# Expert stages: rows of the tokens fetched by index for six of eight pairs of experts, weights in 8 KB pieces, the long conditional inside the sixth pair

## The chip, the cores and the metric

One core of a Trainium2 chip runs the whole program in one launch. The metric is the device time of that launch in microseconds (us). TensorE multiplies, VectorE and ScalarE do the elementwise work and empty the PSUM banks, POOL (GpSimd) does a little of it and starts some DMAs, SP starts the DMAs of the weights. In the profile PE is TensorE, PEld its weight load, DVE VectorE, ACT ScalarE; a name with a q (SPq, PEldq) is the engine's sequencer.

## The reference, cut to what matters

Two transformer blocks of two layers each on 256 tokens of width 1024, all in fp32. The first block's layers end in a mixture of experts; the second block's contain a cross attention to 256 memory tokens with four heads of 64.

```python
def grouped_moe(h, router_w, router_b, w_gate, w_up, w_down):
    scores = sigmoid(t @ router_w)              # 256 tokens x 16 experts, 4 groups of 4
    ...                                         # best group by its top two, then top two experts in it
    top_w = top_s / sum(top_s);  combine = ...  # weight of each expert for each token
    for e in range(16):
        he = silu(t @ w_gate[e]) * (t @ w_up[e])            # 1024 -> 512
        y = y + combine[:, e:e + 1] * (he @ w_down[e])      # 512 -> 1024
```

## The kernel before

**Expert stage** (`moe`, once per layer). The 16 experts are taken as 8 pairs, p = 0 to 7 ("first" to "eighth pair"). All weights of a pair are loaded, 12 pieces of 1 MiB: four each for gate, up and down (`weights`, L1520; `fetch`, L220). Each piece fills one buffer of 128 partitions x 2048 numbers. `fetch` spreads 128 consecutive rows over the partitions, so a partition's 8 KB come in four rows of 2 KB (gate, up) or two of 4 KB (down). 17 buffers take turns; SP issues the DMAs in order and waits for the buffer that comes next to be free. When the stage starts, the buffers are full.

Only tokens that chose an expert are worked on, up to 64 per expert in the main path. From the ranks of the tokens `hot` (L1330) builds a matrix of zeros and ones (tokens x places). `gather` (L1344) picks the tokens on TensorE: the normalised rows, split into a high part `xh` and a low part `xl`, times that matrix, for two pairs at once, column block by column block; ScalarE applies the norm's scale A and bias B on the way out into `hg`. `prepare` (L1379) does it for pairs 0, 2, 4, 6; for pair 0 in two halves, the other times at the end of the pair before.

`up` (L1385) then multiplies `hg` with gate and up weights into banks `pg`, `pu`, two experts side by side in 64 columns each; adds the pair before back to the residual `x` (`self.pending`, four scatters of two matmuls); turns the places (`places`, L1359: `pS`, `pw`); forms silu(pg) * pu in `hd`, transposes it (`hT`, `hidT`). `down` (L1424) multiplies with the down weights into `po`, scales on VectorE and splits into `eo`, which the next pair scatters.

From the third pair on, a count per pair is read into registers, and two conditionals (L1545 ahead of `up`, L1548 ahead of `down`) take the next 32 tokens per expert (`more_up`, `more_down`), with a gather of their own. A conditional is a unit for TensorE, VectorE and ScalarE: each of them branches, drains and goes on.

For tokens beyond that there is one long conditional, `rounds` (L1509), in five nested levels with all experts' code in each. It stands ahead of the eighth pair, between the issue of its gate and up weights and that of its down weights, and SP takes part in it, since it issues DMAs inside.

**Router** (`router`, L1196) prepares weights for the router at the end of each mixer. **Cross attention** (`cross`, L2095, once per layer of the second block) works in steps over two pairs of heads: scores and exp, transposes of the scores (`cpT`), output (`co`, tokens on the partitions). After both, VectorE scales by the softmax sums (`rs`), and `rows_T` transposes the result (`trr`) for the output projection (`op`).

The order within an engine is set by a planner that simulates the engines at build time; calls in `pin` keep their order.

Of the kernel before, what the change touches and what calls it, by code (L numbers as in the profile page):

```python
# [11 lines left out]
F32 = mybir.dt.float32  # L12
# [53 lines left out]
def shape_constants():  # L66
# [15 lines left out]
        ("sum32", i[:, None] % 32 == np.arange(32)[None, :]),  # L82
        ("slots", np.tile(np.arange(1, 257), (P, 1))),
# [36 lines left out]
class Net:  # L120
# [519 lines left out]
    def start(self):  # L640
# [8 lines left out]
        self.one = self.gp.tile([P, 1], F32, name="one")  # L649
        self.rw = self.gp.tile([P, KD, NE], F32, name="rw")  # L650
# [31 lines left out]
    def vectors(self, ap):  # L682
# [7 lines left out]
        yield  # L690
        small(v2[0:96, :], I["sandwich_g_2"].rearrange("l s (k p) -> (l s k) p", p=P))
# [504 lines left out]
    def router(self, l):  # L1196
# [3 lines left out]
        A, B = self.scale_shift(l, 1)  # L1200
        rwa = self.sp.tile([P, KD, NE], F32, tag="gt", name="rwa")
# [12 lines left out]
    def moe(self, l):  # L1214
# [4 lines left out]
        with self.phase(f"moe{l}", MOE_RING, True) as mp:  # L1219
# [32 lines left out]
            def parts(t):  # L1252
                for c in range(2):
                    sl = (slice(None), t, slice(512 * c, 512 * c + 512))
                    pin(nc.scalar.copy(xh[sl], xn[sl]))
                    pin(nc.gpsimd.tensor_tensor(xl[sl], xn[sl], xh[sl].bitcast(F32), op=ALU.subtract))
            for t in range(2):
                for k0 in (0, 4):
                    self.norm_cols(self.norm_turn(self.x, t, k0), hT, t, k0)
                rs[t] = self.norm_rows(self.x, t, xn, t)  # L1260
            parts(0)
# [7 lines left out]
            parts(1)  # L1269
            sel = mp.tile([P, 2, 16], F32, name="sel")  # L1270
# [73 lines left out]
            def gather(oh, hg, k0=0, k1=KD):  # L1344

                n = hg.shape[2]
                per = min(512 // n, 4)
                for b0 in range(k0, k1, per):
                    ph = self.bank([P, per, n], name="ph")
                    for b in range(per):  # L1350
                        for i, (t, xx) in enumerate(((0, xh), (0, xl), (1, xh), (1, xl))):
                            pin(mm(ph[:, b, :], xx[:, t, 128 * (b0 + b):128 * (b0 + b) + 128], oh[t],
                                   start=i == 0, stop=i == 3))
                    for b in range(per):
                        k = b0 + b
                        nc.scalar.activation(hg[:, k, :], ph[:, b, :], AF.Identity,
                                             scale=A[:, k:k + 1], bias=B[:, k:k + 1])
# [21 lines left out]
            def prepare(p, k1=KD):  # L1379

                hg = self.sp.tile([P, KD, 256], F32, tag="xn", name="hg", bufs=1)
                self.first = hot((p, p + 1), 0, 64), hg
                gather(*self.first, 0, k1)

            def up(p, W):  # L1385

                new = p == 0
                if new:
                    prepare(0, 4)
                oh, hg = self.first  # L1390
# [3 lines left out]
                for w, pp in ((W[0], pg), (W[1], pu)):  # L1394
                    for k in range(KD):
                        if new and w is W[0] and k == 4:
                            gather(oh, hg, 4, 8)
                        for j in range(2):
                            pin(mm(pp[64 * j:64 * j + 64, :], hg[:, k, q][:, 64 * j:64 * j + 64], w[j][k // 4][:, k % 4, :],  # L1399
                                   start=k == 0, stop=k == KD - 1, tile_position=(0, 64 * j)))  # L1400

                if self.pending:
# [4 lines left out]
                V.tensor_tensor(hd, hd, pu, op=ALU.mult)  # L1407
                pt = self.bank([P, 4, P], name="hT")
                for k in range(4):
                    self.tr(pt[:, k, :], hd[:, 128 * k:128 * k + 128])  # L1410
                hidT = self.sp.tile([P, 4, P], F32, tag="e2", name="hidT")
                V.tensor_copy(hidT, pt)
                if p in (1, 3, 5):
                    prepare(p + 1)
                return hidT, Sm, ws
# [8 lines left out]
            def down(W, hidT, Sm, ws, last=False):  # L1424
# [13 lines left out]
                def back(n=4):  # L1438
# [20 lines left out]
            def more_up(p, r, W, hidT):  # L1459


                oh = hot((p,), 32 + 32 * r, 32)
                hg = self.sp.tile([P, KD, 64], F32, tag="e1", name="hga")
                gather(oh, hg)
                pp = self.bank([P, 512], name="pgu")
                for gu in ((0, 1),) if W else ((0,), (1,)):
                    w = W[:2] if W else [weights(src, 512, p, self.spare) if c in gu else None
                                         for c, src in enumerate(("exp_w_gate", "exp_w_up"))]
                    for k in range(KD):
                        for c in gu:  # L1470
                            for j in range(2):
                                i = 2 * c + j
                                mm(pp[32 * i:32 * i + 32, :], hg[:, k, 32 * j:32 * j + 32], w[c][j][k // 4][:, k % 4, :],
                                   start=k == 0, stop=k == KD - 1, tile_position=(0, 32 * i))
# [3 lines left out]
                Sm, ws = places([twice[:, t].rearrange("p c s -> p (c s)") for t in range(2)], p, r)  # L1478
                hd = self.sp.tile([P, 512], F32, tag="gt", name="hda")
                nc.scalar.copy(hd, pp)  # L1480
                pt = self.bank([P, 4, P], name="hT")
                for k in range(4):
                    self.tr(pt[:, k, :], hd[:, 128 * k:128 * k + 128])
# [4 lines left out]
            def more_down(p, W, hidT, Sm, ws):  # L1488
                po = self.bank([P, 512], name="po")
                w = W[2] if W else weights("exp_w_down", 256, p, self.spare)  # L1490
                for k in range(4):
                    for i in range(4):
                        j, c = i % 2, i // 2
                        mm(po[32 * i:32 * i + 32, :], hidT[:, k, 32 * j:32 * j + 32],
                           w[j][k // 2][:, k % 2, 512 * c:512 * c + 512], start=k == 0, stop=k == 3,
# [13 lines left out]
            def rounds(r):  # L1509

                with tc.If(left > 32 + 32 * r):
                    for rr, pp in [(1, e) for e in range(FIRST if r == 2 else 0)] + [(r, e) for e in range(8)]:
                        hidT = self.sp.tile([P, 4, 64], F32, tag="e2", name="hidTa")
                        more_down(pp, None, hidT, *more_up(pp, rr, None, hidT))
                    if r < 6:
                        rounds(r + 1)

            engines = (mybir.EngineType.PE, mybir.EngineType.DVE, mybir.EngineType.Activation)

            def weights(src, step, p, into=None):  # L1520
# [4 lines left out]
                t = [self.fetch(raw, w[j][k0:k0 + step, :]) for raw, (j, k0) in zip(into, cut)]  # L1525
                return t[0::2], t[1::2]

            for p in range(8):
                W = [weights("exp_w_gate", 512, p), weights("exp_w_up", 512, p)]
                self.spare = [self.slot([P, 2048]) for i in range(4)]  # L1530
                if p == 7:
                    left = nc.values_load(cnti[0:1, 0:1], min_val=0, max_val=2 * S,
                                          engines=engines + (mybir.EngineType.SP,))
                    rounds(2)
# [808 lines left out]
```

## Time and profile before

| | us |
|---|---|
| median of 3 runs | 1602.48 (1601.62 to 1604.23) |
| profiled execution, its own time | 1602.07 |
| its span | 1600.3 |
| TensorE busy | 1504.7 (94%) |
| VectorE busy | 887.1 (55%) |
| E0: first gate product to last scatter | 212.8 to 466.7 |
| E1: first gate product to last scatter | 622.3 to 856.0 |

Times inside the execution are counted from the span's start. A busy TensorE can hide small waits, since ends of matmuls are modelled. The DMA share is the time of all packets over 16 DMA engines and can pass 1, since packets overlap a little. The more_up path runs once, in E0's fourth pair.

### The profile page before, as it was taken

To read this page: it belongs to the slowest core of one execution; us is meant where nothing else is said; L and a number is where in the kernel's file an instruction comes from. 1 tells how busy PE (TensorE), PEld (TensorE's weight loads), DVE (VectorE), ACT (ScalarE), POOL (GpSimd) and SP (SyncE) were. 2 spreads that over 40 slices of the span, in tenths; PEclk is the share of its full clock that TensorE was granted. 3 is DMA by queue.
4 is the path that set the end of the run, shared out by engine and by line. 5 is a ranking of instruction groups with operands and counts; after the bars stand their busy time and mean duration, and the time that the engine had idled before them with its cause. 6 is when DMAs were issued, how large, how long until landed. Compare 5 with 4: busy or idle time off the path is not lost. (4 is left out here: it accounts for less than half of the span.)

```text
span 1600.3 us, 23014 instructions
## 1 busy us (share of the span) xinstructions
PE 1504.7 (94%) x8845; PEld 1072.0 (67%) x8845; DVE 887.1 (55%) x1704; ACT 679.6 (42%) x1421; POOL 121.4 (8%) x170
## 2 busy tenths in 40 slices
PE   6999999999789999999978999999999999999998
PEld 3766644444349975444425887888887997888887
DVE  3755531122248984222116786766667776766666
ACT  3434421111035653101105355665556666665554
POOL 0320010000000002000001100110000211110000
PEclk9999999999889999999989999999999999999999
DMA  9998999989968799999998632554655542545640
GB/s 357 345 314 294 344 396 391 391 315 393 347 215 273 276 328 366 397 391 392 394 340 277 182 106 93 162 194 162 220 171 161 163 150 84 186 157 186 210 158 27
DMA packets 225758, 412.30 MB, mean 258 GB/s; under 512 B 7705, under 2 KB 91313, under 8 KB 225617
## 3 DMA queue, kind: packets, MB, share of 16 engines
q1 hardware_dynamic: 223040, 403.46, 71.1%
q0 software_dynamic: 2304, 6.98, 1.4%
q8 instruction: 86, 1.41, 0.4%
q14 instruction: 56, 0.45, 0.1%
q10 hardware_dynamic: 272, 0.00, 0.0%
HBM read 409.35 MB, written 1.06 MB: 256 GB/s over the span
## 5 line engine op out<-in xcount | busy, mean ns | idle before, releaser
L229 DVE TENSOR_TENSOR hl<-w,hl 128x1024 fp32r<-128x1024 f32 x280 | 337.2, 1237 | 49.8 <-ACT hl L228 49.4
L228 ACT CAST hl<-w 128x1024 fp32r<-128x1024 f32 x280 | 280.3, 1046 | 33.0 <-DMA w<-in_even_w_in 19.6
L2218 PE MATMUL pgu<-hT,hl 128*128 128x512 f32 x640 | 224.3, 394 | 0.0
L2219 PE MATMUL pgu<-hT,hl 128*128 128x256 f32 x640 | 177.1, 277 | 0.0
L380 PE MATMUL lin<-hl,hThi 128*128 128x256 f32 (+2 forms) x480 | 158.8, 334 | 2.0 <-ACT hl L228 1.3
L381 PE MATMUL lin<-hl,hThi 128*128 128x256 f32 (+2 forms) x480 | 153.6, 321 | 1.9 <-DVE hl L229 1.7
L382 PE MATMUL lin<-hl,hTlo 128*128 128x256 f32 (+2 forms) x480 | 153.1, 320 | 0.4 <-DVE hTlo L557 0.4
L2218 PEld LDWEIGHTS pgu<-hT,hl 128*128 128x128 f32 x640 | 119.9, 187 | 27.8
L1399 PE MATMUL pg<-w,hg 128*64 128x512 f32 x512 | 118.6, 615 | 19.7 <-ACTq L1545 9.2
L1407 DVE TENSOR_TENSOR hd<-hd,pu 128x512 f32<-128x512 f32 x16 | 11.0, 688 | 225.9 <-PE pu L1399 225.9
L1432 PE MATMUL po<-w,hidT 128*64 128x512 f32 x512 | 113.6, 595 | 10.0 <-DVEq L1548 5.8
L2219 PEld LDWEIGHTS pgu<-hT,hl 128*128 128x128 f32 x640 | 120.2, 188 | 2.0
L1399 PE MATMUL pu<-w,hg 128*64 128x512 f32 x512 | 114.9, 593 | 1.9 <-DMA w<-in_exp_w_up 1.9
L380 PEld LDWEIGHTS lin<-hl,hThi 128*128 128x128 f32 x480 | 92.3, 192 | 17.6 <-issue 8.1
L1399 PEld LDWEIGHTS pg<-w,hg 128*64 128x64 f32 x512 | 40.9, 141 | 93.4 <-issue 69.5
L381 PEld LDWEIGHTS lin<-hl,hThi 128*128 128x128 f32 x480 | 92.2, 192 | 11.0 <-DVE hl L229 3.5
L382 PEld LDWEIGHTS lin<-hl,hTlo 128*128 128x128 f32 x480 | 92.1, 192 | 8.0 <-issue 1.7
L1399 PEld LDWEIGHTS pu<-w,hg 128*64 128x64 f32 x512 | 41.1, 137 | 72.7 <-issue 68.0
L1432 PEld LDWEIGHTS po<-w,hidT 128*64 128x64 f32 x512 | 40.4, 137 | 72.8 <-issue 59.5
L1444 DVE SCALAR_TENSOR_TENSOR of<-po,ws,gate 128x512 f32<-128x512 f32 x32 | 23.9, 748 | 104.5 <-PE po L1432 100.6
L1447 ACT CAST eo<-of 128x512 fp32r<-128x512 f32 x32 | 19.8, 617 | 124.7 <-DVE of L1444 124.4
L380 PE MATMUL linc<-hThi,hl 128*128 128x256 f32 x224 | 66.8, 298 | 0.0
(554 smaller groups left out, 2915.0 us busy)
## 6 DMA issues: line engine op xcount, KB each, us to landing
w<-in_exp_w_gate SPq DMA_DIRECT2D x64, 1024.0 KB, 14.9
w<-in_exp_w_down SPq DMA_DIRECT2D x64, 1024.0 KB, 14.2
w<-in_exp_w_up SPq DMA_DIRECT2D x64, 1024.0 KB, 14.2
w<-in_ada_w SPq DMA_DIRECT2D x48, 1024.0 KB, 7.1
w<-in_ffn_wg SPq DMA_DIRECT2D x22, 1024.0 KB, 5.5
w<-in_ffn_wu SPq DMA_DIRECT2D x22, 1024.0 KB, 7.3
w<-in_ffn_wd SPq DMA_DIRECT2D x22, 1024.0 KB, 8.9
w<-in_even_w_in SPq DMA_DIRECT2D x14, 1024.0 KB, 10.1
```

What stands on the lines that cost most here:

```text
L228: pin(self.nc.scalar.copy(w[:, 0], src))
L229: pin(self.nc.vector.tensor_tensor(w[:, 1], src, w[:, 0].bitcast(F32), op=ALU.subtract))
L380: pin(mm(out, lh, rh, start=start, stop=False))
L381: pin(mm(out, lh, rl, start=False, stop=False))
L382: pin(mm(out, ll, rh, start=False, stop=stop))
L1399: pin(mm(pp[64 * j:64 * j + 64, :], hg[:, k, q][:, 64 * j:64 * j + 64], w[j][k // 4][:, k % 4, :], start=k == 0, stop=k == KD - 1, tile_po ...
L1407: V.tensor_tensor(hd, hd, pu, op=ALU.mult)
L1432: pin(mm(po[c][64 * j:64 * j + 64, :], hidT[:, k, 64 * j:64 * j + 64], W[2][j][k // 2][:, k % 2, 512 * c:512 * c + 512], start=k == 0, sto ...
L1444: V.scalar_tensor_tensor(of, po[c], ws, gate[:, cs], op0=ALU.mult, op1=ALU.mult)
L1447: nc.scalar.copy(eh[c], of)
L2218: mm(pp[i], wh[:, k, :], both[:, :, k, :], start=k == 0, stop=False)
L2219: mm(pp[i][:, 0, :], wl[:, k, :], hi[:, k, :], start=False, stop=k == KD - 1)
```

## The change

1. `fetch` gets the pattern of rows as an argument. Expert weights use `(p k) n -> p k n`: a partition gets consecutive rows, 8 KB in one piece. The contraction index is permuted accordingly: `xh`, `xl`, the hidden columns and A, B (as `self.ab`) are read with a stride.
2. For pairs 0 and 1 `gather` stays. The normalised rows are written to HBM (`xd`, 1 MiB, from POOL). 24 matmuls of one column turn ranks into token numbers (`indices`), and POOL fetches rows by these numbers for pairs 2 to 7 (`rows`: 128 rows for the main path, 64 for more_up, 4 KB each). `columns` transposes them, with scale and bias on ScalarE (one half) and VectorE (the other).
3. In `up` two of the four scatters come ahead of the hidden transposes, two after them, then `places`, then `columns` for the next pair.
4. `rounds` goes; `rest` takes its place: one conditional, not nested, with a loop over all 16 experts and both halves of the tokens. It stands in the sixth pair, between the gate and up products and the scatters, behind the issue of the seventh pair's gate and up weights. Its limit is the one of before: 96 tokens for an expert, 64 in the first two pairs.
5. `router` moves A and B to the permuted order: 16 products with 32 x 4 results.
6. Cross attention scales the scores ahead of their transposes and forms the output with its columns on the partitions: 8 products of 64 x 256 in place of 16 of 128 x 64, no `rows_T`.

```diff
-    def fetch(self, raw, src):
-        self.nc.sync.dma_start(raw, src.rearrange("(k p) n -> p k n", p=P))
+    def fetch(self, raw, src, rows="(k p) n -> p k n"):
+        self.nc.sync.dma_start(raw, src.rearrange(rows, p=P))
...
+        for k in range(4):
+            for j in range(4):
+                nc.tensor.matmul(ps[32 * j:32 * j + 32, k, :], pick[:, k, :], v[:, :, :, j].rearrange("p i b -> p (i b)"),
+                                 start=True, stop=True, tile_position=(0, 32 * j))
...
+                    src = xn[sl].rearrange("p (q k) -> p k q", k=4)
+                    pin(nc.scalar.copy(hi, src))
+                    pin(nc.gpsimd.tensor_tensor(lo, src, hi.bitcast(F32), op=ALU.subtract))
...
+            nc.gpsimd.dma_start(xd.rearrange("(t p) d -> p t d", p=P), xn)
...
+            def indices():
+                px = self.bank([P, 16], name="px")
+                for p in range(2, 8):
+                    h, q = (p - 2) // 3, (p - 2) % 3
+                    for c, n, col in ((0, 128, p), (128, 64, 8 + p)):
+                        for t in range(2):
+                            mm(px[0:n, col:col + 1], ones_of[2 * h + t][:, q, c:c + n], self.tok[:, t:t + 1],
+                               start=t == 0, stop=t == 1)
...
+                rows(0, 2)
+                rows(0, 3)
+                rows(1, 2)
+            def rows(i, p):
+                n = 64 if i else 128
+                nc.gpsimd.indirect_dma_start(got[i][0:n, p % 2, :], None, xd[:, :],
+                                             bass.IndirectOffsetOnAxis(ap=idx[0:n, 8 * i + p:8 * i + p + 1], axis=0))
+            def columns(src, n, out):
+                src = src.rearrange("r (b q k) -> r b k q", b=2, k=4)
+                for b in range(2):
+                    pt = self.bank([P, 4, n], name="hgT")
+                    for k in range(4):
+                        self.tr(pt[:, k, :], src[:, b, k, :])
+                    if b:
+                        o = out[:, 4:8, :]
+                        V.tensor_tensor(o, pt, self.ab[:, 0, b, :].unsqueeze(2).to_broadcast([P, 4, n]), op=ALU.mult)
+                        V.tensor_tensor(o, o, self.ab[:, 1, b, :].unsqueeze(2).to_broadcast([P, 4, n]), op=ALU.add)
+                        continue
+                    for k in range(4):
+                        nc.scalar.activation(out[:, k, :], pt[:, k, :], AF.Identity, scale=self.ab[:, 0, b, k:k + 1],
+                                             bias=self.ab[:, 1, b, k:k + 1])
...
+                if between:
+                    between()
+                if p == 0:
+                    indices()
                 if self.pending:
-                    self.pending()
-                Sm, ws = places([oh[t][:, q] for t in range(2)], p, 0)
+                    self.pending(2)
                 hd = self.sp.tile([P, 512], F32, tag="e1", name="hd")
...
+                turn_hidden(hd, hidT)
+                if self.pending:
+                    self.pending(2)
+                Sm, ws = places([oneh[t][:, q] for t in range(2)], p, 0)
+                if 1 <= p < 7:
+                    columns(got[0][:, (p + 1) % 2, :], P, hg[0][:, (p + 1) % 2])
+                    if p < 6:
+                        rows(1, p + 2)
+                    if p < 5:
+                        rows(0, p + 3)
...
-                if p == 7:
...
-                    rounds(2)
...
+            def rest():
+                W.extend(first_two(6))
+                self.spare = [self.slot([P, 2048]) for i in range(4)]
...
+                with tc.If(left > 96):
...
-                own = up(p, W)
+                own = up(p, W, rest if p == 5 else None)
...
-                    V.reciprocal(rs[:, :, h], sm)
+                    V.reciprocal(sm, sm)
+                    for t in range(2):
+                        V.tensor_scalar(p[:, t, :], p[:, t, :], sm[:, t:t + 1], None, op0=ALU.mult)
...
+                o = self.bank([P, S], name="co")
+                for j in range(2):
+                    for b in range(2):
+                        h = 2 * m + b
+                        mm(o[64 * b:64 * b + 64, :], v[:, j, 64 * h:64 * h + 64], st[h][:, j, :], start=j == 0, stop=j == 1,
+                           tile_position=(0, 64 * b))
+                self.finish(oT, o, m)
```

## Rows read from the trace of the kernel before

**Rows 1.** Engine table of the page: busy us, share of the span, instructions.

```profile
PE 1504.7 (94%) x8845; PEld 1072.0 (67%) x8845; DVE 887.1 (55%) x1704; ACT 679.6 (42%) x1421; POOL 121.4 (8%) x170
```

**Rows 2.** Stretches of E1 and E0: busy per engine, granted clock, DMA share, GB/s.

```profile
640.00:820.00 180.00, 166.34 (x813) 76.17 (x812) 44.49 (x71) 27.39 (x62) 0.00 (x0) 1.00 1.04 393
...
337.00:344.00 7.00, 5.01 (x24) 1.90 (x26) 3.85 (x6) 2.45 (x5) 0.00 (x0) 1.00 0.24 90
432.00:441.00 9.00, 5.51 (x16) 1.86 (x18) 0.00 (x0) 0.00 (x0) 0.00 (x0) 0.54 0.62 199
```

**Rows 3.** Waits in E0: who for whom, us in total, times, longest.

```profile
PE po L1432 <- DMA w<-in_exp_w_up: 0.8, 1, 0.8
```

**Rows 4.** Waits in E1, the same columns.

```profile
PE pu L1399 <- DMA w<-in_exp_w_up: 1.9, 2, 1.4
```

**Rows 5.** Timeline of TensorE, fifth to seventh pair of E0, then E1's last down product.

```profile
348.00 7.09 PE L1399 MATMUL pg<-w,hg 128*64 128x512 f32 x32 [0.31 <-PEq L1545]
...
364.30 0.26 PE L1366 MATMUL pw<-cl,kept 128*128 128x16 f32 x1
364.41 0.65 PE L183 MATMUL hT<-kt,hd 128*128 128x128 f32 x4
365.89 7.09 PE L1432 MATMUL po<-w,hidT 128*64 128x512 f32 x32 [0.83 <-DVEq L1548]
373.29 7.09 PE L1399 MATMUL pg<-w,hg 128*64 128x512 f32 x32 [0.30 <-PEq L1545]
...
390.82 0.39 PE L1352 MATMUL ph<-kept,xh 128*128 128x256 f32 x1 [0.47 <-DVE kept L1340]
...
394.74 0.28 PE L1352 MATMUL ph<-kept,xl 128*128 128x256 f32 x1
...
402.81 1.51 PE L1399 MATMUL pg<-w,hg 128*64 128x512 f32 x6 [0.30 <-PEq L1545]
...
845.74 6.21 PE L1432 MATMUL po<-w,hidT 128*64 128x512 f32 x28
```

**Rows 6.** Timeline of TensorE behind the long conditional, in E0 and in E1.

```profile
435.49 9.48 PE L1399 MATMUL pg<-w,hg 128*64 128x512 f32 x32 [7.70 <-ACTq L1511]
...
824.53 1.97 PE L1399 MATMUL pg<-w,hg 128*64 128x512 f32 x4 [9.21 <-ACTq L1545]
```

**Rows 7.** TensorE's jumps at L1511: ns min/median/max, first and last start.

```profile
L1511 PEldq COMPARE_BRANCH  x2: 6215/6229/6243, 423.7 to 811.4; - x2
```

**Rows 8.** SP's DMA issues around the long conditional of E1: start, us until the last.

```profile
810.02 10.89 SPq L221 DMA_DIRECT2D w<-in_exp_w_up  x4
833.91 2.27 SPq L221 DMA_DIRECT2D w<-in_exp_w_down  x4
```

**Rows 9.** Timeline of TensorE: first and last of the 32 gather matmuls of more_up.

```profile
295.14 0.27 PE L1352 MATMUL ph<-oh,xh 128*128 128x64 f32 x1 [2.83 <-DVE oh L1340]
...
300.05 0.40 PE L1352 MATMUL ph<-oh,xl 128*128 128x64 f32 x1
```

**Rows 10.** DMA rate from 640 to 820 us in 40 slices of 4.5 us.

```profile
GB/s 414 399 386 387 387 388 401 411 397 387 386 386 386 395 410 401 386 384 387 387 392 408 403 390 388 385 388 389 410 408 390 383 386 387 391 407 407 390 390 380
```

**Rows 11.** DMA from 833 to 850 us: rate in 40 slices; issues, KB each, landing.

```profile
GB/s 0 0 19 0 135 87 116 414 386 414 434 395 415 443 395 434 405 443 415 424 395 414 434 405 405 424 414 405 405 390 386 386 390 386 381 390 386 414 371 371
...
w<-in_exp_w_down SPq DMA_DIRECT2D x4, 1024.0 KB, 9.0
```

**Rows 12.** Groups of E0 by shape: busy us, mean ns of one, idle before.

```profile
L1407 DVE TENSOR_TENSOR hd<-hd,pu 128x512 f32<-128x512 f32 x8 | 5.5, 688 | 110.8 <-PE pu L1399 110.8
...
L1256 POOL TENSOR_TENSOR xl<-xn,xh 128x512 fp32r<-128x512 f32 x2 | 2.6, 1332 | 0.8 <-ACT xh L1255 0.8
```

**Rows 13.** Timeline of TensorE in the first cross attention: output products to projection.

```profile
1034.32 3.82 PE L2154 MATMUL co<-kv,pT 128*128 128x64 f32 x32
...
1039.99 0.47 PE L380 MATMUL op<-hl,oTh 128*128 128x512 f32 x1
```

More of the change, by code (lines that the diff above doesn't have):

```diff
@@ L1342, in hot, with gather @@
                 return ohs
[L1344 to L1350, printed above, removed]
+            hg = []
+            def gather(k0, k1):
+                if not hg:
+                    hg.append(self.sp.tile([P, 2, KD, P], F32, tag="xn", name="hg", bufs=1))
+                for b0 in range(k0, k1, 2):
+                    ph = self.bank([P, 2, 256], name="ph")
+                    for b in range(2):
@@ L1377, in places, with up @@
                 return Sm, ws
[L1379 to L1390, printed above, removed]
+            def up(p, W, between=None):
+                nonlocal oneh
+                if p == 0:
+                    oneh = hot((0, 1), 0, 64)
+                    gather(0, 4)
+                    tokens_of()
                 q = slice(128 * (p % 2), 128 * (p % 2) + 128)
@@ L1436, in down, with back @@
                 order = [(c, t) for c in range(2) for t in range(2)]
-                def back(n=4):
+                def back(n):
                     for c, t in [order.pop(0) for i in range(n)]:
@@ L1457, in down, with more_up @@
                         self.split_ahead(PRE)
[L1459 to L1464, printed above, removed]
+            def more_up(p, W, hidT):
+                oh = hot((p,), 64, 32)
+                hga = self.sp.tile([P, KD, 64], F32, tag="e1", name="hga")
+                columns(got[1][0:64, p % 2, :], 64, hga)
                 pp = self.bank([P, 512], name="pgu")
[L1466 to L1474, printed above, removed]
+                for k in range(KD):
+                    for i in range(4):
+                        c, j = i // 2, i % 2
+                        mm(pp[32 * i:32 * i + 32, :], hga[:, k, 32 * j:32 * j + 32], W[c][j][k // 4][:, k % 4, :],
+                           start=k == 0, stop=k == KD - 1, tile_position=(0, 32 * i))
                 twice = self.sp.tile([P, 2, 2, 64], F32R, tag="gt", name="ohd")
@@ L1477, in more_up @@
                     V.tensor_copy(twice[:, t], oh[t].unsqueeze(1).to_broadcast([P, 2, 64]))
-                Sm, ws = places([twice[:, t].rearrange("p c s -> p (c s)") for t in range(2)], p, r)
+                Sm, ws = places([twice[:, t].rearrange("p c s -> p (c s)") for t in range(2)], p, 1)
                 hd = self.sp.tile([P, 512], F32, tag="gt", name="hda")
@@ L1486, in more_up, with more_down @@
                 return Sm, ws
-            def more_down(p, W, hidT, Sm, ws):
+            def more_down(W, hidT, Sm, ws):
                 po = self.bank([P, 512], name="po")
-                w = W[2] if W else weights("exp_w_down", 256, p, self.spare)
                 for k in range(4):
@@ L1524, in weights, with first_two @@
                 cut = [(j, k0) for k0 in range(0, w[0].shape[0], step) for j in range(2)]
[L1525 removed]
+                t = [self.fetch(raw, w[j][k0:k0 + step, :], "(p k) n -> p k n") for raw, (j, k0) in zip(into, cut)]
                 return t[0::2], t[1::2]
[L1528 to L1535 removed]
+            def first_two(p):
+                return [weights("exp_w_gate", 512, p), weights("exp_w_up", 512, p)]
@@ L1536, in moe @@
+            oneh, W = None, []
+            for p in range(8):
+                if p != 6:
+                    W = first_two(p)
+                    self.spare = None
+                W = W[-2:] + [weights("exp_w_down", 256, p, self.spare)]
                 if p == 7:
@@ L2108, in cross @@
             oT = ap.tile([P, 2, S], F32R, name="oTh"), ap.tile([P, 2, S], F32R, name="oTl")
-            o = [self.bank([P, 256], name=f"co{t}") for t in range(2)]
-            rs = ap.tile([P, 2, 4], F32, name="rs4")
             st = {}
```

134 lines of the change are left out of this document (93 added, 41 removed).

## Prediction

> **What bounds the kernel now.** I read the engine table first: TensorE is busy 1504.7 us of 1600.3 [rows 1], so outside the expert stages I take a saving on TensorE as a saving of time. The expert stages (E0 in layer 0, E1 in layer 1) need more care, because there the DMA engines are full too: 393 GB/s and packets 1.04 of the time over 180 us of E1 [rows 2]. The waits tell the stages apart. In E0 one line of TensorE waits 0.8 us in all for weights [rows 3], while the DMA engines twice run nearly empty (shares 0.24 and 0.62) because no buffer is free [rows 2]: E0 is bound by TensorE. In E1 TensorE begins to wait for weights, 1.9 us on one line [rows 4]: the two are level, and what TensorE saves there is lost to weights within a few us. So E0 is summed along TensorE, E1 along the DMA.
>
> A pair of experts without a gather runs from 348.00 to 373.29, 25.3 us, 0.83 of it a gap before the down product; the next one, with a gather for two pairs, to 402.81, 29.5 us: 27.4 on average [rows 5].
>
> **The long conditional.** Before, it stands ahead of the eighth pair. TensorE idles 7.70 us there in E0 and 9.21 in E1 [rows 6], and in E0 the gate product behind it takes 9.48 us in place of 7.09 [rows 5, 6] at a granted clock of 0.54 in that stretch [rows 2]: after the idle time it ran partly at 1.2 GHz. Price 10.1 us in E0, about 11.6 in E1, of which 0.3 is usual between pairs [rows 5]. What is waited for is the slowest engine's way past the block: VectorE and ScalarE arrive only after the seventh pair's last work. After, the block stands in the sixth pair behind the gate and up products, where these two have had nothing to do since the pair's start: they can pass it some 10 us ahead of TensorE. TensorE's own jump stays: 6.23 us, begun at 423.7 [rows 7], 4.1 us before its queued products end (435.49 less 7.70 [rows 6]). That leaves 2.2, and 0.4 for draining. Behind them I put 2 us for a lower clock: after a gap of 2.83 us 32 matmuls take 5.3 us [rows 9] where 32 larger ones take 4.2 [rows 5]. So 4.7 us, and a gain of 5.1 in E0; bounds 0 (it costs as much there) and 7.1 (2.7 is all).
>
> The Trainium skill (Runtime: NRT & Kernel Launch, Instruction fetch mechanics) says that a taken branch whose target is not in the fetched window waits for a DMA of instructions. The 6.23 us of the jump agree. By that rule no place is free; if TensorE's queue hid none of it, the gain would be 10.1 less 0.3, 6.2, 0.4 and 2.0, 1.2 us.
>
> SP passes the same block. In E1 it issues the last up pieces from 810.02 on and the next DMA only at 833.91 [rows 8]: it waits until all that it issued has landed. This drain moves from the last four pieces to behind the seventh pair's gate and up weights. The empty time (some 3.4 us, from SP's issue to full rate [rows 11]) is the same in both places: nothing added. Queued behind it are the seventh pair's down weights, which TensorE needs some 20 us later.
>
> **Gathers.** Three gathers per stage go, one for two pairs each: 32 matmuls from 390.82 to 395.0, 4.2 us [rows 5]. Each of six pairs gets 8 transposes, 0.12 us apart (four take 0.65 with one latency [rows 5]): with two changes of bank 1.3 us. ScalarE and VectorE must copy them, at some 0.7 us per pass of 512 columns [rows 12], before the down product: I add 0.8 us of new waiting. The 0.83 gap shrinks to 0.4, because two scatters, the places and the transposes now stand behind the hidden transposes. New pair: 25.3 - 0.8 + 0.4 + 1.3 + 0.8 = 27.0, against 27.4; over six pairs 2.4 us, of which I count 1.5, since the first of them has no conditional and little gap to lose. Bounds 6.3 less (no new wait) and 3.9 more (1.7 us of wait in each: two VectorE passes and the branch).
>
> The one pair in E0 with more than 64 rows gathers again: 32 matmuls, 5.3 us [rows 9], replaced by 8 transposes: 4.1 less. Against it, 24 one-column matmuls for the indices in the first pair, at the 0.11 us spacing of small ones [rows 5] 2.6 us, half of it in a gap that was there: 1.3 more. In the router 16 tiny fp32 products, 32 instructions of 0.06 to 0.11 us: 2 us more per layer, bounds 0 and 3.5. The reordered copies on POOL I cost at nothing, since they end before the first gather; if strided reads doubled their 1.33 us [rows 12], the first gather would start up to 2.7 us later.
>
> E0: - 5.1 - 1.5 - 4.1 + 1.3 + 2.0 = **7.4 us less**.
>
> **DMA.** In E1 the slices alternate between 386 GB/s (gate and up, rows of 2 KB) and 410 (down, 4 KB) [rows 10]: 2.72 and 2.56 us per 1 MiB piece. 256 packets fewer save 0.16 us, so 128 fewer again save 0.08: 2.48 us (423 GB/s) at 8 KB, an estimate. 17 buffers are filled ahead; 79 pieces follow the first freed one, 51 gate or up and 28 down: 51 x 2.72 + 28 x 2.56 = 210 us before, 79 x 2.48 = 196 after. But the rows fetched by index go over the same DMA engines: 6 pairs x 192 rows x 4 KB = 4.5 MiB, 11.5 us at 2.56. So 207.5: 2.8 us less (unrounded 210.3 and 207.5). The write of 1 MiB to HBM falls where the buffers are full anyway. Bounds of a piece: 2.41 (the 434 GB/s of good slices [rows 11]) and 2.72 (length doesn't matter); of the fetched rows: double, 11.5 more.
>
> At the end of E1 the down pieces, issued from 833.91 and a median of 9.0 us under way [rows 8, 11], are all there at about 846.5; TensorE starts on their second half 3.5 us before 851.95, at 848.4 [rows 5]. It is some 1.9 us late, which the cheaper conditional takes back. E1: - 2.8 - 1.9 + 2.0 (router) = **2.7 us less**. Along TensorE alone E1 would lose some 9 us, so weights are what is late next.
>
> The Trainium skill (DMA: Bandwidth & Descriptors, Issuing engines are not separate DMA queues) states that DMAs of every engine run on the same 16 DMA engines and interleave. No row here shows two full queues at once. By the rule the fetched rows are paid in full, as in the sum; were they free, E1 would gain some 6 us more, up to TensorE's bound.
>
> The rows are issued one to two pairs (27 us) ahead of use, and nothing on POOL's queue behind them is needed sooner: I take no wait for them.
>
> **Cross attention**, twice: from the first output product at 1034.32 to the projection at 1039.99, 3.8 us of products and 1.9 of transposes with their waits [rows 13]. After: 8 products in concurrent halves (about 1.8 us) and no transposes, but scaling ahead of the score transposes and a copy chain behind the last product. I take 1 us less each; bounds 2.8 less and 0.5 more.
>
> **Sum:** 7.4 + 2.7 + 2 = 12.1 us less than the profiled execution's 1602.07 us (its span 1600.3; the median of the runs is 0.4 above): **1590 us**.
>
> **Rivals.**
> B, faster: no wait for the new copies, the conditional costs 2.7, pieces take 2.41. E0 - 7.1 - 6.3 - 4.1 + 1.3 + 1 = - 15; E1 saves 5.5 more on the DMA, - 8; cross - 2: 1577. For it: only the order of work on three engines makes these waits; against: at every join now TensorE waits 0.3 to 0.8 us [rows 5].
> C, nearly nothing: the conditional costs as much in the sixth pair, and each pair waits 1.7 us for the copies. E0 0 + 3.9 - 4.1 + 1.3 + 2 = + 3.1; E1 - 2.8 + 2 = - 0.8; cross - 2: 1602.4. For it: the gap before the down product ends on VectorE's queue [rows 5]; against: that queue is empty in the sixth pair.
> D, slower: packet length does not set the rate, pieces take 2.72, and the fetched rows come on top. E1: 79 x 2.72 + 11.5 = 226.4 against 210, + 16.4, + 2 for the router; E0 has DMA time to spare [rows 2] and keeps about half of its 7.4; cross - 2: 1614. It decides from 2.63 us per piece on, where E1 loses the 9.4 us that the others gain. For it: the fast slices are short; against: two rates for two lengths in one stage.
>
> **Numbers.** Forecast (1583 to 1597) 45%, B 22%, C (1597 to 1605) 20%, D 13%. A change of 0.2%, 3.2 us, is what a measurement can tell. Faster: 45 + 22 and a third of C, 74%; within: 13 of C and 1 of D, 14%; slower 12%. Range 1574 to 1604: without the fast end of B, the slow end of C and D.
>
> **What would show it.** Right: no idle TensorE ahead of the eighth pair, one gap of 2 to 3 us in the sixth; pairs of about 27 us; packets of 8 KB near 423 GB/s; E0 shorter by 5 to 10 us, E1 by under 5, with TensorE waiting for weights there. Wrong: E1 shorter by more than E0 (the DMA was cheaper than I think), pairs above 28 us in E0, transposes that wait for fetched rows, a sixth pair above 33 us.

## The result: 0.7% slower, and the profile after

The changed kernel takes 1613.68 us (median of 4 runs, 1611.45 to 1615.67) against 1602.97 beside it: ratio 1.0067, 95% interval 1.0055 to 1.0079. The forecast was 1590, range 1574 to 1604: wrong in sign. Its profiled execution took 1613.21 us, span 1611.4.

The table is worked out from the trace of each kernel. A stage runs from its first transposes (`tr`) to those of the mixer behind it; "late" is the time from the start of the stage to its first gate product. Medians are of all runs of a kernel, stages of one profiled execution each. Ratios are to the kernel before, run beside each (its medians there 1602.43 to 1603.10), with their intervals. Stages whose code is the same differ by 1 to 2 us from trace to trace, the mixer behind E0 by up to 5 (135.6 to 140.6 in the changed kernel and its variants).

| kernel | median us | ratio | E0 | late | E1 | late |
|---|---|---|---|---|---|---|
| before | 1602.97 | 1 | 272.6 | 15.9 | 248.1 | 16.0 |
| changed | 1613.68 | 1.0067 | 267.6 | 23.4 | 260.6 | 23.2 |
| e1, own buffer for hg, 16 weight buffers | 1602.72 | 1.0004 (0.9993 to 1.0014) | 264.0 | 18.7 | 256.4 | 18.9 |
| e1c, 16 weight buffers | 1618.0 | 1.0091 (1.0074 to 1.0108) | 270.4 | 23.4 | 263.5 | 23.4 |
| e2, fewer rows in layer 1 | 1602.22 | 0.9994 (0.9982 to 1.0005) | 268.9 | 23.5 | 248.8 | 22.7 |
| e4, no long conditional | 1597.80 | 0.9964 (0.9953 to 0.9974) | 261.6 | 23.0 | 256.1 | 23.1 |
| e8, the block takes five banks | 1608.24 | 1.0030 (1.0018 to 1.0043) | 265.1 | 23.4 | 260.7 | 23.2 |
| before + 8 KB pieces in layer 1 (e3) | 1595.91 | 0.9956 (0.9943 to 0.9970) | 273.2 | 15.9 | 242.4 | 16.0 |
| before without the conditional (e5) | 1586.28 | 0.9904 (0.9889 to 0.9919) | 262.8 | 15.9 | 242.4 | 16.0 |
| before + cross attention (e6) | 1600.95 | 0.9987 (0.9978 to 0.9996) | 272.5 | 16.0 | 250.0 | 17.5 |
| e1 + empty places left out (e7) | 1588.24 | 0.9906 (0.9893 to 0.9920) | 260.7 | 18.7 | 243.7 | 18.9 |
| e7 + five banks (e9) | 1582.27 | 0.9869 (0.9854 to 0.9885) | 255.6 | 18.9 | 244.1 | 18.7 |
| e9 + contiguous copies (e10) | 1580.74 | 0.9871 (0.9852 to 0.9889) | 254.8 | 18.3 | 243.8 | 18.7 |

E0 did get shorter, by 5.0 us; E1 got 12.5 longer. In between, the mixer of the changed kernel's trace took 140.6 us against 136.8.

The start of E0 in the changed kernel, from the timeline (start, us, engine, line; in brackets the idle time and what ended it):

```profile
205.89 0.80 POOL L1289 DMA_DIRECT2D xd<-xn  x1 [0.85 <-DVE sc L1265]
...
211.52 0.17 PE L1323 MATMUL pr<-pick,b_lexc 128*128 128x16 bf16 x1 [3.40 <-DVE pick L1317]
...
218.65 1.93 ACT L1378 ACTIVATE hg<-ph,ab 128x256 f32<-128x256 f32 x4 [2.33 <-DMA xd<-xn]
...
220.69 5.08 PE L1469 MATMUL pg<-w,hg 128*64 128x512 f32 x16 [5.81 <-ACT hg L1378]
```

ScalarE may write the gathered columns `hg` only when the copy of `xn` to HBM has landed, 12.8 us after POOL issued it, among the weights that fill the DMA engines: `hg` takes over the buffer of `xn`, and the copy reads `xn`. TensorE stands 5.81 us and then begins at the lower clock (granted 0.55 from 220 to 224 us): the first 16 of the 32 matmuls of its gate product take 5.08 us, 3.65 in the kernel before. The buffers are not full while the copy is under way; the DMA engines are still busy filling them (columns as in [rows 2]):

```profile
206.00:218.00 12.00, 5.47 (x35) 3.45 (x33) 9.99 (x35) 2.41 (x4) 3.92 (x3) 0.95 1.01 412
```

The pairs of E0 in TensorE's timeline, against [rows 5, 6]:

```profile
367.16 7.09 PE L1518 MATMUL po<-w,hidT 128*64 128x512 f32 x32 [0.30 <-PEq L1669]
374.63 7.09 PE L1469 MATMUL pg<-w,hg 128*64 128x512 f32 x32 [0.38 <-PEq L1666]
...
394.84 0.76 PE L1505 MATMUL py<-eo,kept 128*128 128x512 f32 x1 [6.26 <-DVEq L1610]
...
400.61 7.09 PE L1518 MATMUL po<-w,hidT 128*64 128x512 f32 x32 [0.30 <-PEq L1669]
408.01 7.09 PE L1469 MATMUL pg<-w,hg 128*64 128x512 f32 x32 [0.30 <-DMA w<-in_exp_w_gate]
...
426.41 7.18 PE L1518 MATMUL po<-w,hidT 128*64 128x512 f32 x32 [0.30 <-PEq L1669]
433.88 6.66 PE L1469 MATMUL pg<-w,hg 128*64 128x512 f32 x30 [0.30 <-PEq L1666]
```

A plain pair takes 25.9 us (408.01 to 433.88) and nothing is idle ahead of the eighth. The sixth takes 33.4, with 6.26 idle at the conditional (L1610) and a granted clock of 0.83 behind it (396 to 401 us). All instructions of that line, by engine (count, ns min/median/max, first and last start):

```profile
L1610 ACTq COMPARE_BRANCH  x2: 45/45/45, 382.1 to 781.5; - x2
...
L1610 PEldq COMPARE_BRANCH  x2: 6018/6064/6111, 384.5 to 786.0; - x2
...
L1610 DVEq COMPARE_BRANCH  x2: 56/56/56, 389.1 to 789.7; - x2
L1610 PEldq EVENT_SEMAPHORE  x2: 51/51/51, 390.6 to 792.1; - x2
L1610 DVEq EVENT_SEMAPHORE  x2: 21/21/21, 394.7 to 795.2; - x2
```

TensorE begins its jump at 384.5, 4 us before its products end at 388.6, and is through at 390.6, as forecast. VectorE comes to the branch only at 389.1 and is behind it at 394.7: TensorE waits for VectorE.

E1, against [rows 2, 4, 10]. First two stretches (columns as in [rows 2]), with the first of them in the kernel before on top:

```profile
620.00:640.00 20.00, 19.80 (x108) 9.53 (x106) 1.63 (x8) 6.58 (x14) 0.00 (x0) 1.00 0.95 337
```

```profile
620.00:640.00 20.00, 15.62 (x70) 8.15 (x70) 4.58 (x19) 5.41 (x10) 0.00 (x0) 0.76 0.50 199
640.00:820.00 180.00, 162.29 (x760) 71.66 (x758) 45.98 (x74) 22.56 (x57) 11.23 (x12) 0.96 0.99 393
```

Then the first half of the first gate product and the waits (us in total, times, longest), the DMA rate in 40 slices from 640 to 820 us with the queues (packets, MB, share of 16 engines), and SP's issues:

```profile
628.72 5.86 PE L1469 MATMUL pg<-w,hg 128*64 128x512 f32 x16 [4.38 <-ACT hg L1378]
```

```profile
PE pu L1469 <- DMA w<-in_exp_w_up: 6.6, 6, 1.4
PE py L1505 <- DVEq L1610: 6.2, 1, 6.2
...
PE pg L1469 <- DMA w<-in_exp_w_gate: 4.0, 1, 4.0
ACT hg L1378 <- DMA xd<-xn: 2.4, 1, 2.4
```

```profile
GB/s 351 424 422 415 331 271 402 421 419 411 398 336 421 424 410 422 364 382 421 415 415 424 330 413 421 424 417 414 427 330 422 422 422 417 413 419 415 413 382 98
...
q1 hardware_dynamic: 9022, 65.65, 91.2%
q0 software_dynamic: 1344, 4.72, 7.5%
```

```profile
798.11 0.33 SPq L222 DMA_DIRECT2D w<-in_exp_w_gate  x1
818.14 2.09 SPq L222 DMA_DIRECT2D w<-in_exp_w_down  x4
```

Between 620 and 640 the DMA engines are half empty (199 GB/s against 337 before): the buffers are full by then, and TensorE, which has to free them, has not begun or runs at the lower clock. From 640 to 820 the rate is the 393 GB/s of before, though the slices now reach 415 to 424; around each fetch of rows they fall to 271 to 398, and 4.72 MB of what moves are rows. SP issues nothing from 798 to 818 (it waits at the conditional for what it issued), and the last slice falls to 98.

### The profile page after: what moved, and what is told of

It reads as the page before. It is cut to its first block, busy times and chain, and to the rows that moved or that the text cites. A ratio compares the mean times of both kernels' runs of the same rounds, so it can differ in the third digit from the quotient of the medians.

```text
span 1611.4 us, 23041 instructions
## 1 busy us (share of the span) xinstructions
PE 1503.6 (93%) x8797; PEld 1066.4 (66%) x8797; DVE 915.2 (57%) x1769; ACT 677.0 (42%) x1417; POOL 148.4 (9%) x196
## 3 DMA queue, kind: packets, MB, share of 16 engines
q0 software_dynamic: 5536, 18.51, 3.5%
HBM read 418.79 MB, written 3.16 MB: 262 GB/s over the span
## 5 line engine op out<-in xcount | busy, mean ns | idle before, releaser
L2337 PE MATMUL pgu<-hT,hl 128*128 128x256 f32 x640 | 178.0, 279 | 0.0
L1518 PE MATMUL po<-w,hidT 128*64 128x512 f32 x512 | 117.0, 609 | 3.8 <-PEq L1669 2.4
L381 PEld LDWEIGHTS lin<-hl,hThi 128*128 128x128 f32 x480 | 94.0, 196 | 18.4 <-issue 7.9
L382 PEld LDWEIGHTS lin<-hl,hThi 128*128 128x128 f32 x480 | 94.1, 196 | 10.8 <-DVE hl L230 3.2
L1447 ACT CAST kept<-pS 128x256 fp32r<-128x256 f32 x17 | 6.3, 372 | 176.5 <-PE pS L184 176.5
```

The lines of the kernel that those rows point to most:

```text
L381: pin(mm(out, lh, rh, start=start, stop=False))
L382: pin(mm(out, lh, rl, start=False, stop=False))
L1518: pin(mm(po[c][64 * j:64 * j + 64, :], hidT[:, k, 64 * j:64 * j + 64], W[2][j][k // 2][:, k % 2, 512 * c:512 * c + 512], start=k == 0, sto ...
L2337: mm(pp[i][:, 0, :], wl[:, k, :], hi[:, k, :], start=False, stop=k == KD - 1)
```

## The experiments

Two readings of the loss came first. The held-write theory: `hg` waits for the copy to HBM, and both stages begin late. The rows theory: the fetched rows fill the DMA engines, and E1 pays for them.

**e1 and e1c: the buffer of hg.** In e1 `hg` gets a buffer of its own. One weight buffer goes to make room; e1c, with the buffer gone and nothing else, is the control.

```diff
-MOE_RING = 2
+MOE_RING = 1
-    hg.append(self.sp.tile([P, 2, KD, P], F32, tag="xn", name="hg", bufs=1))
+    hg.append(mp.tile([P, 2, KD, P], F32, name="hg"))     # not in e1c
```

> Changed kernel, with a buffer of its own for the gathered columns hg, which in the changed kernel take over the buffer of xn; to make room one of the 17 weight buffers goes. Held-write theory: the first pair starts 7 to 9 us late in each stage because hg cannot be written until the copy of xn to HBM has landed. Then the gap of 5.8 us ahead of the first gate product (4.4 in E1) closes to under 0.5, E0 gets 6 to 8 us shorter and E1 7 to 10, less 0 to 3 us per stage for the missing buffer: 1596 to 1603 us against 1613.7. Rival (rows theory): E1 is held by the DMA engines with the fetched rows on them, so a late start costs nothing there, as the buffers are full: E0 6 to 8 shorter, E1 by under 2: 1605 to 1608.

> Changed kernel with 16 weight buffers in place of 17 and nothing else: the control for the run with a buffer of its own for hg. Held-write theory: 1613 to 1619 us (a piece of 2.5 us later per stage at most). The rows theory expects the upper half of that, since weights are what E1 lacks: 1616 to 1621.

E0 is 6.4 us shorter than the control's and E1 7.1; the median falls by 15.3 against the control and 11 against the changed kernel. (The control's stages are those of its shortest execution, 1611.06; its other five took 1615.85 to 1618.84.) So the late start is not absorbed in E1, where the DMA engines are the bound: the buffers are full, nothing moves, and that time does not come back. But the first gate product still comes 2.8 us later in each stage than in the kernel before. In e1's timeline ScalarE waits for TensorE alone, and the first products run at the full rate:

```profile
212.41 0.17 PE L1323 MATMUL pr<-pick,b_lexc 128*128 128x16 bf16 x1 [3.38 <-DVE pick L1317]
...
216.11 1.97 ACT L1378 ACTIVATE hg<-ph,ab 128x256 f32<-128x256 f32 x4 [7.04 <-PE ph L1374]
...
216.95 3.65 PE L1469 MATMUL pg<-w,hg 128*64 128x512 f32 x16
```

**e2: the rows.**

```diff
 def rows(i, p):
+    if l and p > 3:
+        return
```

> Changed kernel; in layer 1 the rows are fetched by index only for the pairs 2 and 3, and the pairs 4 to 7 work on whatever lies in the buffers (their tokens are left out). 768 of 1152 rows go, 9.2 us of the 13.8 us that the packets of the rows take on 16 engines. Rows theory: E1 gets 8 to 12 us shorter: 1602 to 1606. Held-write theory: most of E1's loss comes from the late start, but what then bounds it is the DMA, so the rows that go are regained up to TensorE's bound: 5 to 9 us, 1605 to 1609. If rows travel beside the weights for nothing: under 1 us.

E1 is 11.8 us shorter for 768 of 1152 rows: by that slope, an estimate, all of them cost 17.7. The queues from 640 to 820 us say how:

```profile
q1 hardware_dynamic: 9686, 70.47, 95.7%
q0 software_dynamic: 448, 1.57, 2.6%
```

In the changed kernel the rows take 7.5% of 180 us, 13.5 us for 4.72 MB (2.86 us per MB), and the weights beside them 0.912 x 180 / 65.65 = 2.50 us per MB, where e3 and e7 below show 2.42. Rows are dearer than weights by the byte and slow them too. The Trainium skill (DMA: Bandwidth & Descriptors, Issuing engines are not separate DMA queues) has DMAs of all engines interleave on the same 16; these rows agree, POOL's rows being paid in full and more.

**e3: 8 KB pieces alone,** in layer 1 of the kernel before.

```diff
-t = [self.fetch(raw, w[j][k0:k0 + step, :]) for raw, (j, k0) in zip(into, cut)]
+rows = ("(k p) n -> p k n", "(p k) n -> p k n")[l]
+t = [self.fetch(raw, w[j][k0:k0 + step, :], rows) for raw, (j, k0) in zip(into, cut)]
```

> Kernel before, with the expert weights of layer 1 alone in 8 KB pieces (its contraction runs over permuted rows there, so the experts' results of layer 1 are left wrong; the work is the same). If the length sets the rate: in the kernel before a gate or up piece takes 2.85 us of 16 engines and a down piece 2.64, 220.6 us for the 79 pieces of E1; in the changed kernel a piece takes 2.60, 205.3 for 79. E1 then gains what TensorE waits for weights there, 1.9 us and some 4 us inside two slow up products: 3 to 6 us, 1597 to 1600. If the DMA alone bounds E1: 13 to 15 us, 1588. If the length does not matter: 1602 to 1603.

E1 is 5.7 us shorter. From 640 to 820 us the rate is 413 GB/s against 393 [rows 2], and the queue of the weights reads

```profile
q1 hardware_dynamic: 10166, 73.98, 99.3%
```

0.993 x 180 / 73.98 = 2.42 us per MB, 2.53 per piece of 1 MiB. So length sets the rate, as forecast (2.48), and rival D's premise (2.72) falls. The DMA would allow more: TensorE's waits for weights are gone from E1 in e3 (1.9 us before, [rows 4]), so what is left there has TensorE as its bound.

**e4 and e5: the conditional taken out,** of the changed kernel and of the kernel before.

```diff
-left = nc.values_load(...)
-with tc.If(left > 96): ...      # e5: rounds(2)
```

> Changed kernel without the long conditional (tokens beyond 96 of an expert are left out; there are none in this data). The gap of 6.3 us in the sixth pair of E0 and the 2 to 3 us of half clock behind it go: E0 6 to 9 us shorter. In E1 the DMA engines are full, so TensorE's gap is covered and only the wait of SP counts (3 to 4 us in which the DMA engines run at 258 GB/s): 3 to 4 us. Together 9 to 13 us: 1601 to 1605. A rival in which the block's place in the sixth pair costs as little as forecast (4.7 us in E0, nothing in E1): 1608 to 1610.

> Kernel before without the long conditional ahead of the eighth pair (tokens beyond 96 of an expert are left out; there are none in this data). By the forecast's prices it costs 9.8 us in E0 and 9 to 11 in E1: 1582 to 1585. If it costs in the kernel before no more than in the changed one, where taking it out gave 16 us in the time (6 in E0, 4.5 in E1 and the rest behind them): 1586 to 1592. If E1 is held by the DMA, only the wait of SP counts there, 3 to 5 us: 1588 to 1590.

Ahead of the eighth pair the block costs 9.8 us in E0, the price that the forecast took from the trace, and 5.7 in E1, where TensorE then waits for weights instead (forecast 9 to 11). In the sixth pair, E0 is 6.0 shorter without it and E1 4.5. But the 6.0 are too few for its price. The sixth pair itself, from gate product to gate product, takes 25.8 us in e4 against 33.4:

```profile
377.07 7.09 PE L1469 MATMUL pg<-w,hg 128*64 128x512 f32 x32 [0.30 <-DMA w<-in_exp_w_down]
...
402.87 1.51 PE L1469 MATMUL pg<-w,hg 128*64 128x512 f32 x6 [0.31 <-PEq L1625]
```

So the price in E0 is 7.5 us, and the move gained 2.3 there, not 5.1. What hides the rest is e4's first pair, which takes 30.3 us in place of 27.7 (its down product 8.78 in place of 7.09, with a granted clock of 0.71 from 244 to 248 us). The medians of e4 and of the changed kernel lie 15.9 us apart, more than 6.0 and 4.5: another 5.0 is the mixer behind E0 (140.6 and 135.6 us), where the two have the same instructions. In the changed kernel's trace the granted clock is 0.83 in two stretches of 10 us there (from 534.9 and 564.9), in e4's 1.00 from 469.7 to the end of the mixer; by these rows that is some 3.4 us, an estimate. Why the clock fell there stays open.

**e8: why VectorE comes late to the block.** The block inside takes all eight PSUM banks in turn; `pg` and `pu` sit in two of them, so `hd`, which reads these, has to come first on VectorE, and it waits for the last up product. In e8 the block takes five banks once and uses them over again:

```diff
 with tc.If(left > 96):
+    own = [self.bank([P, 512], name="own") for i in range(5)]
...
-    ps.append(self.bank([P, 512], name="pe"))
+    ps.append(own[len(ps)])
...
-    po = [self.bank([P, 512], name="poe") for c in range(2)]
+    po = own[2:4]      # columns and turn_hidden get own[4]
```

> Changed kernel; the block inside the long conditional uses five PSUM banks over again in place of taking all eight in turn, so that the banks of pg and pu need not be empty ahead of it. Theory: in the changed kernel VectorE's product hd stands ahead of the branch for that reason, waits there for the last up product (388.6) and only then jumps, until 394.7; with the banks free VectorE jumps some 10 us earlier, and what is left is TensorE's own jump (384.5 to 390.5, products until 388.6): the gap of 6.3 us falls to 2 to 2.5, less half clock behind it, E0 4 to 6 us shorter, E1 (bound by the DMA engines) 0 to 2: 1607 to 1610. Rival (the gap is TensorE's and SP's own way past the block): 1613 to 1614.

L1610 and TensorE behind it in e8:

```profile
L1610 DVEq COMPARE_BRANCH  x2: 56/56/56, 379.6 to 764.8; - x2
...
L1610 DVEq EVENT_SEMAPHORE  x2: 21/21/21, 386.0 to 771.4; - x2
L1610 PEldq COMPARE_BRANCH  x2: 5985/6051/6117, 386.7 to 780.8; - x2
```

```profile
392.97 0.77 PE L1505 MATMUL py<-eo,kept 128*128 128x512 f32 x1 [2.24 <-PEq L1610]
```

VectorE is through at 386.0, before TensorE jumps at 386.7, and TensorE waits 2.24 us for its own jump: the forecast's 2.2. The sixth pair takes 29.5 us (376.77 to 406.31) in place of 33.4, 3.9 less. The median falls by 5.4 us, E0 by 2.5 alone (its first pair takes 29.8 us in place of 27.7, as in e4), E1 not at all.

**e6: cross attention alone,** on the kernel before.

```diff
-V.reciprocal(rs[:, :, h], sm)
+V.reciprocal(sm, sm)
+for t in range(2):
+    V.tensor_scalar(p[:, t, :], p[:, t, :], sm[:, t:t + 1], None, op0=ALU.mult)
...
-        mm(o[t][:, sl], st[h][:, t, j, :], v[:, j, sl], start=j == 0, stop=j == 1)
+        mm(o[64 * b:64 * b + 64, :], v[:, j, 64 * h:64 * h + 64], st[h][:, j, :], start=j == 0, stop=j == 1,
+           tile_position=(0, 64 * b))
```

> Kernel before with the cross attention of the changed kernel and nothing else. Forecast: 1 us less each, 1600.5. By the changed kernel's trace, 0.5 us in the first and 1.8 in the second: 1600.2. If the scaling ahead of the transposes costs more than the transposes of the output that go: 1603 or more.

The median is 2.1 us less (0.6 to 3.5 by the interval), in line with the forecast's 2. In the changed kernel's trace, against [rows 13], the first output product stands 3.6 us ahead of the projection in place of 5.7:

```profile
1046.76 1.51 PE L2276 MATMUL co<-pT,kv 128*64 128x256 f32 x10
...
1050.32 0.50 PE L381 MATMUL op<-hl,oTh 128*128 128x512 f32 x1
```

**e7: rows of empty places left out,** on e1.

```diff
-("tok", i[:, None] + 128 * np.arange(2)[None, :]),
+("tok", i[:, None] + 128 * np.arange(2)[None, :] + 1),
...
-V.tensor_copy(idx[:, 2:8], px[:, 2:8])
-V.tensor_copy(idx[0:64, 10:16], px[0:64, 10:16])
+for n, c in ((P, 2), (64, 10)):
+    V.tensor_scalar(none[0:n], px[0:n, c:c + 6], 0.5, 1000.0, op0=ALU.is_lt, op1=ALU.mult)
+    V.scalar_tensor_tensor(idx[0:n, c:c + 6], px[0:n, c:c + 6], -1.0, none[0:n], op0=ALU.add, op1=ALU.add)
...
-                bass.IndirectOffsetOnAxis(...))
+                bass.IndirectOffsetOnAxis(...), bounds_check=S - 1, oob_is_err=False)
```

> Changed kernel with a buffer of its own for hg and 16 weight buffers, and places without a token get an index beyond the last row, so that POOL's fetch leaves them out: about 64 rows a pair in place of 192, since 512 choices are spread over 8 pairs. Rows theory: two thirds of the rows' DMA time go, in E1 9 to 12 us of the 256.4 that the kernel with its own buffer takes there; E0, bound by TensorE, stays: 1590 to 1594 us. If the time of a fetch lies in POOL's issuing and not in the rows moved: 1600 to 1603.

E1 is 12.7 us shorter than e1's, the median 14.5. E0 is 3.3 shorter too, which was not expected and stays open. From 640 to 820 us:

```profile
q1 hardware_dynamic: 9798, 71.36, 95.8%
q0 software_dynamic: 1346, 1.71, 2.7%
```

1.71 MB in place of 4.72, and the weights are back at 0.958 x 180 / 71.36 = 2.42 us per MB. With e2 this settles E1: it is the rows moved, not POOL's issuing, that cost.

**e9 and e10: all together.** e9 is e7 with e8's five banks. In e10 VectorE writes `xn` in the permuted order at once, so that the copies to `xh` and `xl` are contiguous:

```diff
-rs[t] = self.norm_rows(self.x, t, xn, t)
+rs[t] = self.mean_square(self.x, t)
+V.tensor_scalar(xn[:, t, :].rearrange("p (c k q) -> p c k q", c=2, k=4),
+                self.x[:, t, :].rearrange("p (c q k) -> p c k q", c=2, k=4), rs[t], None, op0=ALU.mult)
...
-pin(nc.scalar.copy(hi, src))
+pin(nc.scalar.copy(xh[sl], xn[sl]))
```

> The kernel that leaves out empty places in the fetch, with its own buffer for hg, and now with five banks for the block in the long conditional. Theory of the banks: E0 4 to 6 us shorter than its 260.7, E1, no longer far from TensorE's bound, 2 to 5 shorter than 243.7: 1579 to 1583. Rival: no more than the changed kernel gains by the same edit in E0 alone: 1584 to 1588.

> The kernel before it, and the normalised rows are written in the permuted order by VectorE at once, so that the copies on ScalarE and POOL are contiguous again (ScalarE's 1.11 us against 0.61 in the kernel before). Theory: the 2.8 us that the first gate product is late even with a buffer of its own for hg (18.7 us after the stage's first transposes, 15.9 in the kernel before) come from these copies: E0 2 to 3 us shorter, E1 1 to 3: 3 to 5 us less than the run with skipped places and five banks. Rival: VectorE's strided pass takes the time instead: within 1 us of it.

e9 beats the kernel before by 1.3% and the changed one by 31 us. The five banks give 5.1 us in E0 here and nothing in E1, where 2 to 5 were expected. e10 is level with e9: the strided copies were not what keeps its start late. Its timeline:

```profile
207.52 2.85 DVE L1299 TENSOR_TENSOR ec<-sel 128x128 f32<-128x128 f32 x1
207.72 2.48 POOL L1272 TENSOR_TENSOR xl<-xn,xh 128x512 fp32r<-128x512 f32 x2
...
210.75 0.18 DVE L1298 TENSOR_TENSOR gc<-gs 128x32 f32<-128x32 f32 x1
...
212.03 0.17 PE L1323 MATMUL pr<-pick,b_lexc 128*128 128x16 bf16 x1 [3.16 <-DVE pick L1317]
```

## Why the prediction was wrong, step by step

- **The write to HBM (0 forecast).** This is the step that failed. "The write of 1 MiB to HBM falls where the buffers are full anyway" looked only at what the write costs the DMA engines. That it reads `xn`, whose buffer `hg` takes next, was overlooked, though both kernels give `hg` that buffer. It cost 6.4 us in E0 and 7.1 in E1 (e1 against e1c, both with 16 weight buffers; against the changed kernel with its 17, e1 is 3.6 and 4.2 shorter). Nor were the buffers full: the DMA share from 206 to 218 us is 1.01, and the copy took 12.8 us to land. In the kernel before, too, it stays at 1.03 to 1.05 from the start of E1 (606.3) to 624 us, so the buffers are not full when the stage starts, but only some 18 us later.
- **The router and its copies (2.0 a layer, the copies nothing).** The router's 16 products take 0.66 us in the trace, ahead of the stage's start, which is 0.4 us later than before. The lateness lies behind them: without the held buffer the first gate product is still 2.8 us late (18.7 against 15.9). The size is within the bounds, 3.5 for the router and 2.7 for the copies, but the reason is not the copies' strides, since contiguous ones (e10) did not take it away. In E0 of e1 some 0.7 us of it come ahead of the router's last products (`rlT`), 0.9 are the longer wait ahead of `pr` (3.38 in place of 2.53), and 1.2 come behind that wait, where the gather runs at a lower clock than before (kernel before, then e1; the last three columns are granted clock, DMA share, GB/s):

```profile
210.50:212.80 2.30, 2.30 (x18) 2.05 (x16) 0.99 (x8) 0.98 (x3) 0.00 (x0) 1.00 1.04 386
```

```profile
214.00:216.90 2.90, 2.90 (x18) 2.73 (x16) 2.90 (x10) 0.79 (x2) 0.00 (x0) 0.71 1.02 422
```

- **The fetched rows (11.5 us).** They cost 17.7 by e2's slope. They were priced as weights by the byte; they take 2.86 us per MB and slow the weights from 2.42 to 2.50.
- **Pieces (2.48 us).** e3 measured 2.53, within the bounds: this step was right.
- **The conditional (4.7 us left of 10.1).** The price ahead of the eighth pair was right (10.1 less 0.3; measured 9.8), and so were TensorE's own 2.2 (e8). But 7.5 were left in the sixth pair: VectorE could not "pass it some 10 us ahead", since the block needs the banks that its own waiting product has to empty. The forecast's own sign of being wrong, a sixth pair above 33 us, came (33.4).
- **Gathers (pair 27.0).** A pair took 25.9, since each of the gaps was shorter than forecast. From the second pair's gate product to the eighth's the kernel before takes 189.9 us without the conditional (e5), and the changed one 185.5, which is 178.0 without its 7.5: 11.9 less, where the forecast had 1.5 for the gathers and 4.1 for the more_up path.
- **Cross attention (2).** e6 measured 2.1. In the changed kernel's own trace it is not to be seen: all that stands behind E1 takes 745.3 us against 745.9.

E0 by its pairs: the first gate product comes 7.5 us later, the first pair is 2.3 longer, the next six are 11.9 shorter without the conditional, the conditional is 2.3 cheaper and the rest 0.6 shorter. That makes the 5.0 less of the table; 7.4 less had been forecast, so the gathers, mis-sized in the good direction, covered most of the late start.

E1 by sums: forecast - 2.7, measured + 12.5, so 15.2 missed. The first gate product is 7.2 us later and its first half takes 5.86 in place of 3.65 us, 9.4 in all, of which 2.0 stood in the sum; the rows add 6.2 over the forecast. That is 13.6 of 15.2. The sum doesn't close: 0.05 us more for each of 79 pieces would be another 4.0, and with these it is 2.4 too much. The other miss in the whole is the mixer behind E0, 3.8 us in this one trace.

Of the rivals, D named 1614, but by pieces that stay slow, which e3 refutes; the right end for a wrong reason. The forecast that weights are what E1 lacks next was right for the middle of E1 and wrong for its start: with the buffers full, a late consumer idles the DMA engines.

## What to carry to other kernels

Before a new reader of a tile is costed by its bytes, ask which tile takes over that buffer and when it is written: a transfer that nobody waits for can hold the next owner. In a stage bound by the DMA engines a consumer that starts late with full buffers costs its whole delay (7.1 us here), and rows fetched for empty places cost like real ones. A conditional that is not taken still reserves what its body uses; the fewer buffers it shares with the work around it, the earlier each engine can pass.

## What the runs showed of the hardware that was not expected

- The body of a block that is never entered decided when VectorE came to its branch: at 389.1 us where the body takes all eight banks, at 379.6 where it takes five, for the same place in the program.
- Fetched rows whose index lies beyond the bound move no bytes, but the count of packets stays. The software queue over the whole run, e7:

```profile
q0 software_dynamic: 5536, 12.51, 2.5%
```

in the changed kernel 5536 packets, 18.51 MB and 3.5%.

- A small comparison on VectorE takes long beside POOL's subtraction. In the changed kernel `gc` takes 1.52 and 1.55 us while POOL makes its two passes, in e10's timeline above 0.18 once POOL is done:

```profile
207.24 3.23 POOL L1274 TENSOR_TENSOR xl<-xn,xh 128x512 fp32r<-128x512 f32 x2 [0.56 <-ACT xh L1273]
207.53 1.52 DVE L1298 TENSOR_TENSOR gc<-gs 128x32 f32<-128x32 f32 x1
208.97 1.55 DVE L1299 TENSOR_TENSOR gc<-gs 128x32 f32<-128x32 f32 x1
```

The Trainium skill (SBUF — State Buffer, SBUF: two separate sides) calls the port pair of the two engines an exclusive lock that one holds for a whole instruction. The 1.5 us, about one pass of POOL (3.23 for two), agree. In e10 `ec` takes 2.85 us, longer than both passes (2.48 together), which a lock of one instruction alone does not explain. Faster copies left this delay, and TensorE's wait of 3.16 us ahead of `pr`, as they were.

- TensorE's granted clock: in E1 of the changed kernel it is 0.76 from 620 to 640 us, where the engine had stood still ahead of the first gate product and then ran its first half at the lower of the two levels (1.2 of 2.4 GHz); a late start is paid twice. Over the whole execution it is 0.973 to 0.975 in the four runs of the changed kernel and 0.977 to 0.983 in the twelve of e1, which starts earlier.
